# Writing out the order of three engines from a LayerNorm's last sum into the next product, in a two-layer encoder trunk

## The chip, the cores and the metric

The kernel runs on one core of a Trainium2 chip. The metric is the device time of one execution in microseconds (us), the median of several runs. Five engines work side by side, each through its own list of instructions in order: TensorE (PE in the profile; PEld is its weight loads), VectorE (DVE), ScalarE (ACT), GpSimd (POOL) and SyncE (SP), which here only issues DMA transfers.

## What is computed

A sequence of 256 frames of width 2048 goes through two post-norm layers. In short:

```python
h = layer_norm(x, ln_in_g, ln_in_b)
for l in range(2):
    z = h @ w_in[l]                       # queries, keys/values, rope part, conv input u
    u = u + b_glu; c = u[:, :1024] * sigmoid(u[:, 1024:])
    c = silu(layer_norm(depthwise_conv(c, 31 taps)))
    mix = concat([chunk_causal_attention(z), c]) @ w_out[l]
    h = layer_norm(ALPHA * h + mix, ln1_g[l], ln1_b[l])
    f = square(relu(h @ w1[l])) @ w2[l]   # 2048 -> 8192 -> 2048
    h = layer_norm(ALPHA * h + f, ln2_g[l], ln2_b[l])
```

All in float32; positions give the rotary angles of a part of queries and keys.

## The kernel before

**Splitting.** A float32 product is made of three products of a shorter type (float32r): a number is split into hi, its cast, and lo, the rest. ScalarE makes hi, VectorE or GpSimd subtracts to get lo (`split`, L170, and `cutting`, L248, for weights). `stat_x` (L352) then issues, for one 128-row slice `ki`, the products xh·hi, xh·lo, xl·hi into one bank of PSUM.

**Tiling.** The frames are two tiles of 128 (t = 0, 1); the width is four blocks of 512 (n, or kc when it is summed over). A weight chunk is 512 rows by 512 columns (1 MB, four `ki` slices): loaded by SP into a raw buffer `wr`, cut into `wh` and `wl`, used once by each tile t, then dropped. `pump` (L282) keeps a few chunks cut ahead (`ahead`) and some loaded ahead (`cap`), out of 20 big buffers. `gpsimd_low` (L42) says for which chunks GpSimd makes lo.

**Norm.** `accumulate` (L712) adds a product's bank to X and takes the block's statistics; `Norm.head` (L397) aggregates them, with a power on GpSimd (`rstd_of`, L365). `Norm.nrm` (L409) normalises a block in two operations on VectorE (subtract mean and multiply by g; multiply by r and add b), or in two on ScalarE and two on GpSimd. `Norm.turn` (L432) transposes a block on TensorE (four 128x128) and splits the result into xT (tiles `xTa`, `xTb`; `xTi` for the input norm).

**Into the next product.** `close` (L725) writes the last product of a norm's sum; amid it `between` (L727) sums and normalises tile 0's blocks and turns the first. With two chunks of activations (the `wo` case, L741) blocks 2 and 3 are written interleaved, so that tile 0 is summed early. `after_norm` (L448) then writes the other turns and the first product, chunk by chunk. No order is written down there: the scheduler of the build decides how norm, turns, products and cuts of weights are interleaved on each engine. This happens three times: `wo` to `w1` in both layers, and `w2` of layer 0 to `u` of layer 1. The last norm (`N.last`) has no product behind it.

**The opening** (L519 to L581). 24 small products without use (`warm`) come first; x is normalised by a `First` norm (L487) without gain, turned, and gain and bias are applied by ScalarE or VectorE as the turned block leaves PSUM (`gain`, L497; `GV`, L52, lists VectorE's share), into `xv`, which is split into `xTi`. The first product `u` (layer 0, group 0: four chunks, two tiles, banks `u000` and `u001`) follows; then small parameters are transposed (`parameters`, L594: `prmT`, `wdT`), and the product `zq` starts. The small parameters come through SP's queue (L540 to L551), ahead of the fifth weight chunk.

Of the kernel before, what the change touches and what calls it, by code (L numbers as in the profile page):

```python
# [16 lines left out]
P = 128  # L17
D = 2048
S = 256
# [32 lines left out]
GV = {(t, n, k) for t, n in ((1, 0), (1, 1), (0, 2)) for k in range(4)} | {(0, 0, 2), (0, 0, 3)}  # L52
# [24 lines left out]
def hybrid_trunk(ctx: ExitStack, tc: tile.TileContext, x, positions, inv_freq, ln_in_g, ln_in_b,  # L77
# [3 lines left out]
    clock = dict(pe=0.0, dve=0.0)  # L81

    class Counted:

        def __init__(self, eng, key, cost):
            self.eng, self.key, self.cost = eng, key, cost
# [26 lines left out]
    vector = Counted(nc.vector, "dve", dve_cost)  # L113

# [55 lines left out]
    def split(hi, lo, src):  # L170
        return nc.scalar.copy(hi, src), vector.tensor_sub(lo, src, hi.bitcast(F32))  # L171
# [76 lines left out]
    def cutting(pieces):  # L248
# [7 lines left out]
        eng = nc.gpsimd if gpsimd_low(plan[i][0]) else vector  # L256
        for j in range(pieces):
            c = slice(j * m, (j + 1) * m)
            with ExitStack() as order:
# [4 lines left out]
                nc.scalar.copy(hi[:, c], raw[:, c])  # L264
                low = eng.tensor_sub(lo[:, c], raw[:, c], hi[:, c].bitcast(F32))  # L265
                if eng is nc.gpsimd:
                    last["low"] = low
# [97 lines left out]
    def rstd_of(var, eps, scale, name):  # L365
# [3 lines left out]
        nc.gpsimd.tensor_tensor(out=r, in0=v, in1=mhalf, op=ALU.pow)  # L369
        return r  # L370

    class Norm:
        def __init__(self, name, g_ap, b_ap, last=False):
# [5 lines left out]
            self.turned = set()  # L379
# [28 lines left out]

        def nrm(self, t, n, eng=None):  # L409
# [7 lines left out]
            if eng is nc.gpsimd:  # L417
                nc.scalar.activation(X[:, t, c], a, AF.Identity, bias=self.nmu(t), scale=1.0)  # L418
                nc.scalar.activation(X[:, t, c], X[:, t, c], AF.Copy, scale=r)  # L419
# [12 lines left out]
        def turn(self, t, n):  # L432
            if (t, n) in self.turned:
                return
            self.turned.add((t, n))
            while len(self.xT) <= n:
                self.xT.append(v3(big(f"xT{self.name}{len(self.xT)}", F32R), 4))
            xt = self.xT[n]
# [3 lines left out]
            ps = self.gain(ps, t, n)  # L442
            self.cut = split(xt[:, :, t * P:(t + 1) * P], xt[:, :, S + t * P:S + (t + 1) * P], v3(ps, 4))
# [4 lines left out]
    def after_norm(N, keys, ps, lag):  # L448

        def mm(t, kc):  # L450
            hi, lo = get(*keys[kc])
            for ki in range(4):
                stat_x(ps[t], hi, lo, ki, N.xT[kc][:, ki], t, kc == 0 and ki == 0, kc == 3 and ki == 3)
                yield

        state["hold"] = True
        for n in range(3):
            N.nrm(0, n)
            N.turn(0, n)
        N.nrm(1, 0)  # L460
        N.turn(1, 0)
        gate = N.cut
        N.nrm(0, 3)
        N.turn(0, 3)
        for n in range(1, NC4):
            N.nrm(1, n)
            N.turn(1, n)
# [5 lines left out]
        for kc in range(lag):  # L473
            for _ in mm(1, kc):
                pass
            tick()
            retire(*keys[kc])
        for kc in range(lag, NC4):
            for t in range(2):
                for _ in mm(t, kc):  # L480
                    pass
                tick()
            retire(*keys[kc])
        state["gate"] = None


    class First(Norm):  # L487

# [8 lines left out]
        def gain(self, ps, t, n):  # L497
            v = work(f"xv{t}{n}", "ev", 4)
            for k in range(4):
# [4 lines left out]
                else:  # L504
                    nc.scalar.activation(v[:, c], ps[:, c], AF.Identity, bias=b, scale=g)
            return v

# [31 lines left out]
    with nc.allow_non_contiguous_dma(reason="one position a partition"):  # L539
        nc.sync.dma_start(posi, positions[0].rearrange("(t p) -> p t", p=P))  # L540
    nc.sync.dma_start(invf, inv_freq.partition_broadcast(P))
# [3 lines left out]
    for l in range(L):  # L545
        o = l * NR
        for r0, nr, ap in ((0, 16, b_glu), (16, 8, g_cln), (24, 8, b_cln), (32, 8, b_dw)):
            nc.sync.dma_start(prm[o + r0:o + r0 + nr, :], ap[l].rearrange("(r c) -> r c", c=P))
    wdr = big("wdr")
    for l in range(L):  # L550
        nc.sync.dma_start(wdr[:CK, l * CW:(l + 1) * CW], w_dw[l])  # L551
# [3 lines left out]
    nc.scalar.copy(gbT, ps[:, 0:32])  # L555

    def ready_tile(t, n):
        N.nrm(t, n)
        N.turn(t, n)

# [3 lines left out]
    first = cutting(4)  # L564
    next(first)
    next(first)
    ready_tile(0, 0)
    state["gate"] = N.cut[:1]
    beside(first)
    state["gate"] = None  # L570
    ready_tile(0, 1)
    for n in range(NC4):
        N.stats(1, n)
    N.head(1)
    ready_tile(1, 0)
    for n in range(1, NC4):
        for _ in cutting(4):
            pass
        if n + 1 < NC4:
            ready_tile(0, n + 1)  # L580
        ready_tile(1, n)  # L581
# [12 lines left out]
    def parameters():  # L594
# [3 lines left out]
        nc.scalar.copy(pT.rearrange("p l r -> p (l r)"), ps[:, 0:NR * L])  # L598
        nc.scalar.mul(pH.rearrange("p l r -> p (l r)"), ps[:, 0:NR * L], 0.5)
        for l in range(L):  # L600
# [4 lines left out]
            nc.scalar.copy(wdT[:, l].rearrange("p c k -> p (c k)"), ps[:, 0:8 * CK])  # L605
# [28 lines left out]
    def rope_tables():  # L634
        af, tmp = angles[:, 0], angles[:, 3]
        nc.scalar.activation(tmp, af, AF.Abs)
        nc.scalar.activation(sinT.rearrange("p a b -> p (a b)"), af, AF.Sin)
        nc.scalar.activation(cosT.rearrange("p a b -> p (a b)"), tmp, AF.Sin, bias=hpi, scale=-1.0)
# [14 lines left out]
    def convolve(l, i, h, ca):  # L653

        acc = [psumc(f"cv{l}{i}{j}", j)[:, :S] for j in range(2)]
        for j in range(2):
            c = 2 * i + j
            nc.scalar.activation(acc[j], h[:, c], AF.Identity, bias=pT[:, l, 32 + c:33 + c],  # L658
# [9 lines left out]
        for j in range(2):  # L668
            nc.scalar.copy(ca[:, 2 * i + j], acc[j])
# [55 lines left out]
    def close(tag, l, k0, act, N, first=False):  # L725

        def between(i, ps):  # L727
            if i == 0:
                accumulate(0, ps, NC4 - 1, first, N)
                N.head(0)  # L730
                N.nrm(0, 2, nc.gpsimd)
                N.nrm(0, 0)
                N.nrm(0, 1)
            elif not N.last:
                N.turn(0, 0)

        if len(act) > 2:
            for n in range(NC4):
                end = n == NC4 - 1
                ps = out_rows(tag, l, k0, n, act, (3 if N.last else 2) if end else 0, between)  # L740
                for t in range(2):  # L741
                    if t or not end:
                        accumulate(t, ps, n, first, N)
        else:
            for n in range(NC4 - 2):
                ps = out_rows(tag, l, k0, n, act)
                for t in range(2):
                    accumulate(t, ps, n, first, N)
# [516 lines left out]
```

## Time and profile before

| | |
|---|---|
| median of 3 runs | 2019.65 us (2018.78 to 2022.06) |
| the profiled execution's own time | 2019.18 us |
| its span | 2017.4 us |
| busy: TensorE, VectorE, ScalarE, GpSimd | 98%, 61%, 47%, 17% of the span |
| mean granted clock of TensorE | 0.994 of full |
| read from HBM | 373.88 MB, 186 GB/s over the span |

The profile shows one execution. Its page gives busy time by engine and, in 40 slices of the span, the granted clock of TensorE. A timeline has one row for a run of like instructions on an engine: start, length, engine, line, operation, output and inputs, count, and in brackets how long the engine was idle before and what ended that. A matmul's row lasts from its start to its modelled end, so that matmuls overlap: the pace of TensorE is read from start to start. L93 is a helper through which all TensorE and VectorE instructions go.

### The profile page before, as it was taken

Reading aid. Unit: us, or ns where it says so; the run is one execution under the profiler, and the core shown is the slowest. Engines: PE = TensorE matmul, PEld = TensorE weight load, DVE = VectorE, ACT = ScalarE, POOL = GpSimd, SP = SyncE. Lnnn points to the kernel's source line nnn. Section 1 sums busy time; section 2 is a strip of 40 time slices with the busy share of each in tenths; the row PEclk is TensorE's granted clock in tenths of the full one; section 3 lists DMA queues with packets and bytes.
Section 4 is the critical chain, followed back from the end, with each engine's and each line's share of the span. In section 5 each row is a group of like instructions: output and inputs, shape, how many; then the busy total and the mean of one; then the engine's idle time right before and its main releaser. Section 6 shows DMA issues by size and latency. Waiting matters only on the chain. (4 is left out here: it accounts for less than half of the span.)

```text
span 2017.4 us, 26187 instructions
## 1 busy us (share of the span) xinstructions
PE 1984.3 (98%) x10542; PEld 1708.7 (85%) x10542; DVE 1223.8 (61%) x1725; ACT 946.9 (47%) x1341; POOL 333.6 (17%) x208
## 2 busy tenths in 40 slices
PE   7999999999999999999999999999999999999998
PEld 5999878888888888888879997788888888888886
DVE  6875687554555555466567747865555555555564
ACT  5456455543453354344345464555444434543441
POOL 2287902000000000000038764200000000000001
PEclk7999999999999999999999999999999999999999
DMA  7565746456555645657556455455564565556562
GB/s 228 157 168 169 258 170 209 148 196 216 171 188 188 229 154 197 213 168 250 167 168 177 135 178 210 167 187 178 198 217 159 189 198 197 186 190 227 190 221 72
DMA packets 226170, 377.67 MB, mean 187 GB/s; under 512 B 15955, under 2 KB 70083, under 8 KB 225025
## 3 DMA queue, kind: packets, MB, share of 16 engines
q1 hardware_dynamic: 225696, 375.47, 56.7%
q8 instruction: 82, 1.34, 0.3%
q10 hardware_dynamic: 352, 0.54, 0.1%
q14 instruction: 40, 0.32, 0.0%
HBM read 373.88 MB, written 2.10 MB: 186 GB/s over the span
## 5 line engine op out<-in xcount | busy, mean ns | idle before, releaser
L264 ACT CAST wh<-wr 128x1024 fp32r<-128x1024 f32 (+2 forms) x700 | 684.9, 1031 | 745.3 <-DVE wl L93 331.6
L93 DVE TENSOR_TENSOR wl<-wr,wh 128x1024 fp32r<-128x1024 f32 (+1 forms) x592 | 694.9, 1216 | 413.0 <-ACT wh L264 289.5
L93 PE MATMUL w<-wh,h 128*128 128x512 f32 x2048 | 632.0, 389 | 1.5 <-DVE f015s L93 1.5
L93 PE MATMUL f<-xTa,wh 128*128 128x512 f32 x1920 | 454.8, 390 | 0.0
L93 PEld LDWEIGHTS w<-wh,h 128*128 128x128 f32 x2048 | 384.5, 188 | 81.4 <-DVE f015s L93 1.7
L93 PEld LDWEIGHTS f<-xTa,wh 128*128 128x128 f32 x1920 | 354.3, 188 | 70.0
L93 PE MATMUL w<-wl,h 128*128 128x512 f32 x1024 | 398.4, 389 | 0.0
L265 POOL TENSOR_TENSOR wl<-wr,wh 128x1024 fp32r<-128x1024 f32 (+1 forms) x108 | 245.1, 2294 | 85.5 <-ACT wh L264 31.4
L93 PEld LDWEIGHTS f<-xTa,wl 128*128 128x128 f32 x1920 | 243.7, 191 | 7.9
L93 PE MATMUL f<-xTa,wl 128*128 128x256 f32 x1920 | 247.3, 283 | 0.0
L369 POOL TENSOR_TENSOR rb<-vb,mhalf 128x1 f32<-128x1 f32 x4 | 3.7, 924 | 1387.0 <-DVE nmub L93 1387.0
L93 PEld LDWEIGHTS w<-wl,h 128*128 128x128 f32 x1024 | 192.3, 188 | 39.5
L93 DVE SCALAR_TENSOR_TENSOR cv<-hg,wdT,cv 128x255 f32<-128x255 f32 (+14 forms) x480 | 187.3, 464 | 11.3 <-ACT cv L658 11.3
L93 PE MATMUL wo<-wh,mx 128*128 128x512 f32 x256 | 82.7, 396 | 1.0 <-ACT mx L171 1.0
L93 PE MATMUL wo<-wh,mc 128*128 128x512 f32 x256 | 79.7, 390 | 0.0
L93 PE MATMUL u<-xTi,wh 128*128 128x256 f32 x384 | 71.4, 286 | 0.0
L93 PE MATMUL u<-xTb,wh 128*128 128x256 f32 x384 | 71.2, 286 | 0.0
L93 DVE TENSOR_TENSOR X<-X,w 128x512 f32<-128x512 f32 x44 | 30.3, 688 | 64.6 <-PE w L93 64.6
L93 PEld LDWEIGHTS u<-xTi,wh 128*128 128x128 f32 x384 | 60.3, 192 | 0.2
L93 PEld LDWEIGHTS u<-xTb,wh 128*128 128x128 f32 x384 | 60.2, 191 | 0.2
L93 PEld LDWEIGHTS wo<-wh,mx 128*128 128x128 f32 x256 | 48.0, 188 | 11.3 <-ACT mx L171 1.5
L93 PEld LDWEIGHTS wo<-wh,mc 128*128 128x128 f32 x256 | 48.1, 188 | 9.9
(403 smaller groups left out, 1811.4 us busy)
## 6 DMA issues: line engine op xcount, KB each, us to landing
wr<-in_w_dram SPq DMA_DIRECT2D x256, 1024.0 KB, 5.2
wr<-in_w_out_dram SPq DMA_DIRECT2D x32, 1024.0 KB, 5.3
wr<-in_w_in_dram SPq DMA_DIRECT2D x60, 512.0 KB, 4.3
wr<-in_w_in_dram SPq DMA_DIRECT2D x8, 1024.0 KB, 11.1
wr<-in_w_uq_dram SPq DMA_DIRECT2D x24, 256.0 KB, 4.3
wr<-in_w_in_dram SPq DMA_DIRECT2D x8, 640.0 KB, 4.1
wr<-in_w_ukv_dram SPq DMA_DIRECT2D x8, 512.0 KB
wr<-in_w_in_dram SPq DMA_DIRECT2D x16, 128.0 KB, 4.8
```

The costliest lines, as they stand in the source:

```text
L93: return f(*args, **kw)
L264: nc.scalar.copy(hi[:, c], raw[:, c])
L265: low = eng.tensor_sub(lo[:, c], raw[:, c], hi[:, c].bitcast(F32))
L369: nc.gpsimd.tensor_tensor(out=r, in0=v, in1=mhalf, op=ALU.pow)
```

## The change

1. A helper (`Counted`) can now chain an engine's instructions in the order in which the program text writes them (`chained`, through `issue_after`), and ScalarE goes through it too. The chain is on for TensorE, VectorE and ScalarE from `between(0)` (or from the opening's start) to the end of the written sequence.
2. `after_norm` is one written sequence. A token is an operation: `f`, `s` the two halves of the norm of block (t, n), `t` its transposes, `p` its split, `a`, `b` the two halves of its product (six matmuls each), `m` all of it, `c` half a cut of the fourth chunk, `x` the rest of it. A turn stands amid a product's twelve matmuls. ScalarE and GpSimd no longer normalise, except in the last norm.
3. `close` no longer has the interleaved `wo` case: tile 0's last two chunks of block 3 come first, then tile 1's.
4. The opening is written in order likewise. The first two chunks of `u` are not cut: their 16 matmuls take the unsplit float32 `xv` and raw weights (16 where 48 were). `GV` gives ScalarE more of the gains.
5. The small loads move from SP's queue to GpSimd's, behind the second power of the input norm; `prmT` and `wdT` wait for the opening's last matmul, the angles for a later power, the rope tables for a later ScalarE instruction.
6. The key rope's transposes move behind `u` group 2; lo of layer 1's `u` group 1 moves from GpSimd to VectorE.

```diff
@@ gpsimd_low, GV, Counted
     if tag == "u":
-        return key[2] >= 2 - l
+        return key[2] >= 2
...
-GV = {(t, n, k) for t, n in ((1, 0), (1, 1), (0, 2)) for k in range(4)} | {(0, 0, 2), (0, 0, 3)}
+GV = {(t, n, k) for t, n in ((1, 1), (1, 3)) for k in range(4)}
...
                 clock[self.key] += self.cost(op, args, kw)
-                return f(*args, **kw)
+                with ExitStack() as order:
+                    if self.key in chained and self.prev is not None:
+                        order.enter_context(tc.issue_after(self.prev.ins))
+                    self.prev = f(*args, **kw)
+                return self.prev
@@ after_norm
-        for n in range(3):
-            N.nrm(0, n)
-            N.turn(0, n)
...
-        for kc in range(lag):
-            for _ in mm(0, kc):
-                pass
-            tick()
-        state.update(hold=False, gate=gate)
...
+        fourth = cutting(2, True)
...
+        for w in ("a00 t01 p01 b00 f02 s02 a01 t02 f10 p02 s10 b01 f11 s11 a02 t10 p10 b02 f12 s12 a10 t11 p11 b10 f03 s03 "
+                  "c a11 t12 p12 b11 c f13 s13 a12 t03 p03 b12 x a03 t13 p13 b03 m13").split():
...
+            if w == "x":
...
+                state["gate"] = (scalar.prev, vector.prev)
...
+        chained.clear()
+        state["hold"] = False
+        pump(index[keys[3]] + 3)
@@ opening
-    nc.sync.dma_start(invf, inv_freq.partition_broadcast(P))
...
-    first = cutting(4)
...
-    for n in range(1, NC4):
-        for _ in cutting(4):
-            pass
-        if n + 1 < NC4:
-            ready_tile(0, n + 1)
-        ready_tile(1, n)
+    chained.update(("pe", "dve", "act"))
...
+            if kc < 2:
+                tensor.matmul(ups[t], lhsT=N.v[t, kc][:, ki * P:(ki + 1) * P], rhs=raw[kc][1][:, ki],
+                              start=kc == 0 and ki == 0, stop=False)
+            else:
+                stat_x(ups[t], *ready[index["u", 0, 0, kc]], ki, N.xT[kc][:, ki], t, False, kc == 3 and ki == 3)
...
+    for step in ("n00 n01 t00 t01 m00 n02 n03 t02 s0 s1 s2 s3 h p00 t03 p01 a01 n10 n11 t10 b01 n12 n13 p02 p03 a10 c2 c2 "
+                 "t11 b10 c2 c2 p10 c3 c3 a11 t12 b11 c3 c3 p12 a02 t13 b02 p11 m12 m03 p13 m13").split():
...
+    small.enter_context(tc.issue_after(last["pow"].ins))
+    for l in range(L):
+        nc.gpsimd.dma_start(wdr[:CK, l * CW:(l + 1) * CW], w_dw[l])
...
+            nc.gpsimd.dma_start(prm[o + r0:o + r0 + nr, :], ap[l].rearrange("(r c) -> r c", c=P))
@@ close, between
+                if not N.last:
+                    state["hold"] = True
+                    chained.update(("pe", "dve", "act"))
                 accumulate(0, ps, NC4 - 1, first, N)
                 N.head(0)
-                N.nrm(0, 2, nc.gpsimd)
-                N.nrm(0, 0)
-                N.nrm(0, 1)
...
+                    for n in range(2):
+                        N.first(0, n)
+                    for n in range(2):
+                        N.second(0, n)
             elif not N.last:
                 N.turn(0, 0)
+                N.parts(0, 0)
@@ layers
         if l == 0:
-            parameters()
+            with tc.issue_after(opened.ins):
+                parameters()
```

**TensorE in the opening.** Names: `tri` and two digits is the turn of block (t, n); `u000`, `u001` the banks of tiles 0 and 1; `wr` raw, `wh`/`wl` cut weights. Before:

```order
L93 MATMUL gbT_158<-ident_109,gbr_106 128x32
L93 MATMUL tri00_179<-ident_109,X_70 128x128 x4
L93 MATMUL tri01_197<-ident_109,X_70 128x128 x4
L93 MATMUL tri02_244<-ident_109,X_70 128x128 x4
L93 MATMUL u000_344<-wh0_171,xTi0_178 128x512
L93 MATMUL u000_344<-wl0_172,xTi0_178 128x512
L93 MATMUL u000_344<-wh0_171,xTi0_178 128x512 x2
...
L93 MATMUL u000_344<-wh1_232,xTi1_196 128x512
L93 MATMUL tri10_220<-ident_109,X_70 128x128 x4
L93 MATMUL tri11_257<-ident_109,X_70 128x128 x4
L93 MATMUL tri03_281<-ident_109,X_70 128x128 x4
```

Now:

```order
L98 MATMUL gbT_146<-ident_109,gbr_106 128x32
L98 MATMUL tri00_163<-ident_109,X_70 128x128 x4
L98 MATMUL tri01_173<-ident_109,X_70 128x128 x4
L98 MATMUL u000_159<-wr0_114,xv00_168 128x512 x4
L98 MATMUL tri02_189<-ident_109,X_70 128x128 x4
L98 MATMUL tri03_212<-ident_109,X_70 128x128 x4
L98 MATMUL u000_159<-wr1_127,xv01_178 128x512 x2
L98 MATMUL tri10_229<-ident_109,X_70 128x128 x4
L98 MATMUL u000_159<-wr1_127,xv01_178 128x512 x2
L98 MATMUL u001_160<-wr0_114,xv10_234 128x512 x2
L98 MATMUL tri11_257<-ident_109,X_70 128x128 x4
L98 MATMUL u001_160<-wr0_114,xv10_234 128x512 x2
```

The product no longer waits for the split: it starts behind two turns, on raw weights and `xv`, and turns stand between halves of products instead of in groups of three behind two whole chunks.

**GpSimd in the opening**, now, behind the two powers of the input norm (before, none of these loads stood in this list):

```order
L377 TENSOR_TENSOR ri0_157<-vi0_155,mhalf_71 128x1
L377 TENSOR_TENSOR ri1_207<-vi1_205,mhalf_71 128x1
L636 DMA wdr_144<-in_w_dw_dram 31x1024
L639 DMA gbr_106<-in_b_glu_dram 16x128
L639 DMA gbr_106<-in_g_cln_dram 8x128
L639 DMA gbr_106<-in_b_cln_dram 8x128
L639 DMA gbr_106<-in_b_dw_dram 8x128
L636 DMA wdr_144<-in_w_dw_dram 31x1024
L639 DMA gbr_106<-in_b_glu_dram 16x128
L639 DMA gbr_106<-in_g_cln_dram 8x128
L639 DMA gbr_106<-in_b_cln_dram 8x128
L639 DMA gbr_106<-in_b_dw_dram 8x128
```

Ten loads stand in one row there; TensorE's `prmT` and `wdT` need them, and stand ahead of `zq`.

**TensorE from `wo` to `w1` in layer 0.** `tra0` and two digits is the turn of block (t, n), `wo0_8_3_1` the last bank of the sum (tile 1), `f000` the next product's bank of tile 0. Before:

```order
L93 MATMUL wo0_8_3_1_3041<-wh44_2941,mc01_2329 128x512
L93 MATMUL tra000_3085<-ident_109,X_70 128x128 x4
L93 MATMUL tra001_3123<-ident_109,X_70 128x128 x4
L93 MATMUL tra002_3131<-ident_109,X_70 128x128 x4
L93 MATMUL f000_3120<-wh45_2973,xTa00_3084 128x512
L93 MATMUL f000_3120<-wl45_2974,xTa00_3084 128x512
L93 MATMUL f000_3120<-wh45_2973,xTa00_3084 128x512 x2
```

Now:

```order
L98 MATMUL wo0_8_3_1_2955<-wh44_2888,mc01_2277 128x512
L98 MATMUL tra000_3025<-ident_109,X_70 128x128 x4
L98 MATMUL wo0_8_3_1_2955<-wh44_2888,mc01_2277 128x512
L98 MATMUL wo0_8_3_1_2955<-wl44_2889,mc01_2277 128x512
L98 MATMUL wo0_8_3_1_2955<-wh44_2888,mc01_2277 128x512 x2
L98 MATMUL wo0_8_3_1_2955<-wl44_2889,mc01_2277 128x512
L98 MATMUL wo0_8_3_1_2955<-wh44_2888,mc01_2277 128x512
L98 MATMUL f000_3046<-wh45_2920,xTa00_3024 128x512
L98 MATMUL f000_3046<-wl45_2921,xTa00_3024 128x512
```

The first turn moved ahead of the last six matmuls of the sum, and the second behind the first six of the next product; three turns in a row stood there before.

**VectorE at the same place** (`X<-X,mva00,ga0` is the first half of a block's norm, `X<-X,ra00,ba0` the second, `xTa00<-tra000` a split's lo, `X<-X,wo0_8_3_1` the last sum). Before:

```order
L93 SCALAR_TENSOR_TENSOR X_70<-X_70,mva00_3025,ga0_2786 128x512 x3
L93 BN_STATS sta01_2785<-X_70 128x6
L93 SCALAR_TENSOR_TENSOR X_70<-X_70,ra00_3029,ba0_2787 128x512 x3
L93 TENSOR_TENSOR X_70<-X_70,wo0_8_3_1_3041 128x512
L93 BN_STATS sta01_2785<-X_70 128x6
L93 TENSOR_TENSOR xTa00_3084<-tra000_3085,xTa00_3084 128x4x128
L93 TENSOR_TENSOR xTa01_3122<-tra001_3123,xTa01_3122 128x4x128
L93 BN_AGGR mva01_3100<-sta01_2785 128x2
```

Now:

```order
L98 SCALAR_TENSOR_TENSOR X_70<-X_70,mva00_2996,ga0_2734 128x512 x2
L98 SCALAR_TENSOR_TENSOR X_70<-X_70,ra00_3000,ba0_2735 128x512 x2
L98 TENSOR_TENSOR xTa00_3024<-tra000_3025,xTa00_3024 128x4x128
L98 TENSOR_TENSOR X_70<-X_70,wo0_8_3_1_2955 128x512
L98 BN_STATS sta01_2733<-X_70 128x6
L98 BN_AGGR mva01_3040<-sta01_2733 128x2
L98 TENSOR_SCALAR va01_3042<-mva01_3040 128x1
L98 TENSOR_TENSOR xTa01_3058<-tra001_3059,xTa01_3058 128x4x128
L98 SCALAR_TENSOR_TENSOR X_70<-X_70,mva00_2996,ga0_2734 128x512
L98 SCALAR_TENSOR_TENSOR X_70<-X_70,ra00_3000,ba0_2735 128x512
L98 SCALAR_TENSOR_TENSOR X_70<-X_70,mva01_3040,ga0_2734 128x512
L98 TENSOR_TENSOR xTa02_3080<-tra002_3081,xTa02_3080 128x4x128
```

The first split's lo now stands ahead of the last sum, and each further split between norm halves of later blocks.

## Rows read from the trace of the kernel before

**Rows 1.** The page: span, and TensorE's share

```profile
span 2017.4 us, 26187 instructions
...
PE 1984.3 (98%) x10542; PEld 1708.7 (85%) x10542; DVE 1223.8 (61%) x1725; ACT 946.9 (47%) x1341; POOL 333.6 (17%) x208
```

**Rows 2.** Windows, opening: length; busy PE, PEld, DVE, ACT, POOL (x); clock; DMA share, GB/s

```profile
12.60:22.70 10.10, 7.95 (x20) 6.00 (x21) 7.82 (x16) 4.11 (x9) 3.42 (x8) 0.50 0.93 289
...
26.20:29.50 3.30, 0.24 (x2) 0.24 (x3) 3.30 (x9) 1.75 (x4) 2.79 (x6) 1.00 0.50 90
29.70:39.80 10.10, 7.98 (x24) 6.04 (x23) 7.32 (x16) 9.10 (x24) 0.93 (x3) 0.50 0.95 311
```

**Rows 3.** Costliest TensorE groups from 8.6 to 54.6 us: busy, mean ns, idle before

```profile
L93 PE MATMUL u<-wh,xTi 128*128 128x512 f32 x64 | 24.9, 469 | 0.9 <-DVE xTi L93 0.9
L93 PE MATMUL u<-wl,xTi 128*128 128x512 f32 x32 | 14.8, 464 | 0.0
L93 PE MATMUL tri<-ident,X 128*128 128x128 f32 x32 | 6.2, 340 | 7.4 <-DVE xv L93 7.2 <-DVE X L93 0.2
```

**Rows 4.** Timeline of the opening: start, length, engine line op, idle before

```profile
6.78 1.28 ACT L264 ACT_TABLE_LOAD   x1 [6.78 <-DMA wr<-in_w_in_dram]
...
8.43 1.91 DVE L93 TENSOR_SCALAR X<-X,mvi,ri 128x512 f32<-128x512 f32 x4 [0.67 <-POOL ri L369]
...
9.89 2.21 ACT L505 ACTIVATE xv<-tri,gbT 128x128 f32<-128x128 f32 x6
...
13.57 1.87 DVE L93 BATCH_NORM_STATS2 sti<-X 128x6 f32<-128x512 f32 x3
...
16.31 2.18 ACT L264 CAST wh<-wr 128x512 fp32r<-128x512 f32 x4 [0.96 <-DMA wr<-in_w_in_dram]
...
22.66 0.58 POOL L369 TENSOR_TENSOR ri<-vi,mhalf 128x1 f32<-128x1 f32 x1
...
24.66 1.03 PE L93 MATMUL tri<-ident,X 128*128 128x128 f32 x8
```

**Rows 5.** Timeline, TensorE after the opening: product at full clock, then zq

```profile
43.29 1.07 PE L93 MATMUL u<-wh,xTi 128*128 128x512 f32 x4
44.20 0.39 PE L93 MATMUL u<-wl,xTi 128*128 128x512 f32 x1
...
53.36 1.18 PE L93 MATMUL wdT<-ident,wdr 31*128 31x31 f32 x16
...
54.66 0.47 PE L93 MATMUL zq<-wh,xTi 128*128 128x512 f32 x1
```

**Rows 6.** Timeline, TensorE in attention: float32 products, two records each

```profile
179.62 0.59 PE L93 MATMUL sc<-qr 128*128 128x256 f32 x2
180.06 0.59 PE L93 MATMUL sc<-kn,qn 128*128 128x256 f32 x2
```

**Rows 7.** Timeline, SP queue: issues of the small loads

```profile
17.93 1.71 SPq L548 DMA_DIRECT2D gbr<-in_b_glu_dram  x1
...
22.52 0.27 SPq L548 DMA_DIRECT2D gbr<-in_g_cln_dram  x1
```

**Rows 8.** The three turns from norm to product, by stretch (columns as rows 2)

```profile
306.37:312.86 6.49, 4.99 (x28) 3.80 (x26) 6.01 (x12) 3.10 (x6) 1.51 (x2) 1.00 1.03 382
1018.48:1025.34 6.86, 5.23 (x28) 3.78 (x26) 6.62 (x11) 2.62 (x5) 2.99 (x3) 1.00 1.06 383
1296.51:1302.91 6.40, 5.20 (x27) 3.79 (x26) 6.33 (x11) 2.42 (x5) 2.35 (x3) 1.00 1.03 384
```

**Rows 9.** Timeline of the middle one: last sum, the two norm halves

```profile
1013.24 0.69 DVE L93 TENSOR_TENSOR X<-X,w 128x512 f32<-128x512 f32 x1 [6.19 <-PE w L93]
...
1015.11 2.07 DVE L93 SCALAR_TENSOR_TENSOR X<-X,mvb,gb 128x512 f32<-128x512 f32 x3
...
1017.10 4.13 DVE L93 SCALAR_TENSOR_TENSOR X<-X,rb,bb 128x512 f32<-128x512 f32 x3
1017.10 1.89 POOL L420 TENSOR_TENSOR X<-X,gb 128x512 f32<-128x512 f32 x1 [0.83 <-ACT X L419]
```

More of the change, by code (lines that the diff above doesn't have):

```diff
@@ L80, in hybrid_trunk @@
     nc = tc.nc
-    clock = dict(pe=0.0, dve=0.0)
+    clock = dict(pe=0.0, dve=0.0, act=0.0)
+    chained = set()
     class Counted:
         def __init__(self, eng, key, cost):
-            self.eng, self.key, self.cost = eng, key, cost
+            self.eng, self.key, self.cost, self.prev = eng, key, cost, None
         def __getattr__(self, op):
@@ L368, in rstd_of @@
         r = sm.tile([P, 1], F32, name=f"r{name}", tag="r")
[L369 removed]
+        last["pow"] = nc.gpsimd.tensor_tensor(out=r, in0=v, in1=mhalf, op=ALU.pow)
         return r
@@ L378, in __init__ @@
             self.done = set()
-            self.turned = set()
+            self.read = {}
             self.xT = []
@@ L563, in hybrid_trunk, with whole @@
     N.head(0)
-    first = cutting(4)
[L565 to L576, printed above, removed]
-        for _ in cutting(4):
-            pass
-        if n + 1 < NC4:
-            ready_tile(0, n + 1)
-        ready_tile(1, n)
+    ups = [psum(f"u00{t}") for t in range(2)]
+    def whole():
+        i = state["cut"]
+        state["cut"] += 1
+        (a, b), _ = plan[i][1]
+        return i, v3(raws.pop(i)[:, :a * b], a)
@@ new lines, in hybrid_trunk @@
+    for step in ("n00 n01 t00 t01 m00 n02 n03 t02 s0 s1 s2 s3 h p00 t03 p01 a01 n10 n11 t10 b01 n12 n13 p02 p03 a10 c2 c2 "
+                 "t11 b10 c2 c2 p10 c3 c3 a11 t12 b11 c3 c3 p12 a02 t13 b02 p11 m12 m03 p13 m13").split():
+        a, b = [int(i) for i in (step[1:] + "00")[:2]]
+        if step[0] == "s":
+            N.stats(1, a)
+        elif step == "h":
+            N.head(1)
+        elif step[0] == "c":
+            next(chunk[a])
+        elif step[0] in "mab":
+            product(a, b, dict(m=range(4), a=(0, 1), b=(2, 3))[step[0]])
+        else:
+            dict(n=N.nrm, t=N.turn, p=N.parts)[step[0]](a, b)
@@ new lines, in hybrid_trunk @@
+    for c in chunk.values():
+        beside(c)
+    chained.clear()
+    opened = tensor.prev
+    small = ExitStack()
+    small.enter_context(tc.issue_after(last["pow"].ins))
+    for l in range(L):
+        nc.gpsimd.dma_start(wdr[:CK, l * CW:(l + 1) * CW], w_dw[l])
+        o = l * NR
+        for r0, nr, ap in ((0, 16, b_glu), (16, 8, g_cln), (24, 8, b_cln), (32, 8, b_dw)):
+            nc.gpsimd.dma_start(prm[o + r0:o + r0 + nr, :], ap[l].rearrange("(r c) -> r c", c=P))
+    with nc.allow_non_contiguous_dma(reason="one position a partition"):
+        nc.gpsimd.dma_start(posi, positions[0].rearrange("(t p) -> p t", p=P))
@@ L762, in close @@
+                N.parts(0, 0)
+        for n in range(NC4):
+            end = n == NC4 - 1
+            ps = out_rows(tag, l, k0, n, act, (3 if N.last else 2) if end else 0, between)
+            for t in range(2):
+                if t or not end:
+                    accumulate(t, ps, n, first, N)
         N.head(1)
-        for n in range(1, NC4):
-            if not N.last or n == 2:
-                N.nrm(1, n, nc.gpsimd)
+        if N.last:
+            N.nrm(1, 2, nc.gpsimd)
     for l in range(L):
```

275 lines of the change are left out of this document (147 added, 128 removed).

## The prediction

> **What bounds the kernel now.** I read the page first. TensorE is busy for 98% of the span [rows 1], so nothing but time that TensorE loses can be won: its idle time, its time at half clock, and its own work. The profiled execution took 2019.18 us, 0.47 below the median of 2019.65; every sum is made against it. Next I read TensorE's pace from start to start: four 512-column products of the split type take 44.20 - 43.29 = 0.91, so 0.2275 us each at full clock [rows 5]. Where the distance between two starts is longer, time is lost. That happens in two kinds of places which the change touches.
>
> First the opening. The windows show the granted clock at 0.50 from 12.6 to 22.7 and from 29.7 to 39.8, that is 1.2 instead of 2.4 GHz [rows 2]. Ahead of these falls TensorE stood: its turns waited 7.2 us for `xv`, the gained block that leaves PSUM [rows 3], and from 26.2 to 29.5 it was busy for 0.24 us of 3.3 [rows 2]. Gain, normalisation and cut of the second tile are made in long runs on VectorE and ScalarE, and three turns stand in a row behind them. The first product's last matmul ends at 53.36, and `zq` starts at 54.66 behind `wdT`, 16 small transposes of 1.18 us in all [rows 5].
>
> Second, the three places where a norm meets the next product. The windows from the first turn to the first half product show 6.49, 6.86 and 6.40 us [rows 8]; each holds twelve transposes and fourteen products. Four transposes take about 0.5 us (eight took 1.03 [rows 4]), so the work is 1.5 + 14 x 0.2275 = 4.7, and 1.8, 2.2 and 1.7 are lost, 5.7 together. VectorE and ScalarE are the reason: the timeline of the middle one shows three second halves of the norm at 4.13 us while GpSimd normalised too, against 2.07 for three first halves [rows 9].
>
> **The opening, added up.** Only the chain of the new order is needed, with durations of these rows. VectorE normalises the first two blocks from 8.43 on, 0.48 each [rows 4]. ScalarE's table load of 1.28 us [rows 4] now falls behind the first small transpose, so that its first gain starts at about 10.4; a gain takes 2.21 / 6 = 0.37 [rows 4]. The product therefore starts at about 10.9. What TensorE has then to do: sixteen unsplit products, which appear as two records of 256 columns in attention at 180.06 - 179.62 = 0.44 for 256 columns [rows 6], so 0.88 for 512, 14.1 together; 48 split ones at 0.2275, 10.9; six turns of 0.5, 3.0. That is 28.0, or 38.9 without a wait. (Sixteen unsplit products replace 48 split ones; this alone costs 14.1 - 10.9 = 3.2.) I see two waits. The second raw chunk lands at 16.3 (the cut in the rows waited for it until then [rows 4]), when TensorE, with four products and two more turns done, has been ready since about 15.3: 1.0. The turn of tile 1's first block needs its normalisation. Its statistics, four of 0.62, can start at about 12.3, and GpSimd's power of 0.58 [rows 4] is done at about 16.6. But in VectorE's list two splits now stand ahead of it, and they need ScalarE: two runs of four gains and two casts of 0.55 to 0.6 (four casts took 2.18 [rows 4]), to 19.1; then a lo of about 0.69 [rows 9] and 0.48: 20.3. TensorE ran dry at 18.0, so 2.4. With both waits the last matmul ends at 42.3. Twelve more handovers between engines are not counted; I take **43**. `zq` follows 1.6 later as before (`prmT`, `wdT` and the two transposes of `uT` between): 44.6 against 54.66. Gain **10.1**. By the bounds of no wait at all (38.9) and no half clock avoided (one fall, below) it lies between 14.2 and 5.
>
> **The small loads.** They leave SP's queue, which frees it for the fifth chunk, and ten of them stand on GpSimd behind the power at 16.6. TensorE's `prmT` and `wdT` now wait for them directly ahead of `zq`, and behind `zq` everything is queued. No row shows a load issued by GpSimd. On SP their issue took 0.27 to 1.71 us [rows 7]; ten at 1.71 would be issued by 33.7, and 5 us more to land still end before 43. So I cost them at nothing; the cover is gone at (43 - 16.6 - 5) / 10 = 2.1 us each. The angles, on the same queue, are needed much later.
>
> A page speaks against this part. The Trainium skill, "SBUF — State Buffer", sections "SBUF: two separate sides" and "A bandwidth-pool intuition that's wrong (but worth ruling out)", says that a transfer issued by GpSimd starves for its descriptors while VectorE runs an operation in a two-port mode: about 3.1 us instead of 0.62. By that figure ten loads would land at about 52.6 and the total would be some 9.6 us above the sum below; no run here shows it yet.
>
> **The three boundaries.** The last sums of tile 0, their statistics, power and two blocks' norm (0.69 + 0.7 + 1.4 for two first halves, the power beside them, + 1.4 for two second ones [rows 9]) take 4.2 us, and TensorE has 18 products, 4.1 us, before the first turn, now put before the last six matmuls of the sum: a wait near zero. From there a turn and twelve products, 0.5 + 12 x 0.2275 = 3.2 us, alternate. In that time VectorE has a first half, a second half and a lo, 3 x 0.69 = 2.1 us with GpSimd quiet, and about 0.65 of waiting for ScalarE's cast: 2.7. So TensorE should set the pace. I leave 0.3 per place for handovers: 5.7 - 0.9 = **4.8** gained, between 0 (another wait in its place) and 6.5 (losses behind the window go as well). The interleaved end of `wo` that is removed had given tile 0's sum its lead; the new order of the last two chunks gives it the same. The cut of the fourth chunk in halves, the shifted cuts behind it and the last split of tile 1, which stands behind five cuts, cost nothing as long as later chunks' products lie between; ScalarE, which no longer normalises, has that time. Moving the key rope's transposes and one group's lo from GpSimd to VectorE (61% busy [rows 1]) costs nothing either.
>
> **Sum:** 2019.18 - 10.1 - 4.8 = **2004.3**.
>
> **Rivals.**
> *B, the clock falls once more in the opening.* TensorE was idle in stretches ahead of both falls [rows 2, 3], and the new order keeps idle times of 1.0 and 2.4 us. One stretch of 10.1 us at half clock costs at most 5.1 of work, less the about 1 us of wait that it covers: 4. Total 2008.3; with nothing gained at the boundaries 2013.1. Against: no idle stretch of the new chain is as long as the 3.3 in the rows.
> *C, the loads are late.* VectorE's second halves took twice as long beside GpSimd [rows 9]; if GpSimd's issues suffer alike, 1.71 doubles to 3.4: the last lands at 16.6 + 34 + 5 = 55.8, 12.8 after the need, total 2017. Below 2.1 us each it vanishes; from 4.1 each the kernel is slower than before. Only the long one of the SP rows speaks for it, the short one (0.27) against.
> *D, slower: VectorE's turn outlasts TensorE's.* In the written order VectorE's lo waits for ScalarE's cast and blocks the norm halves behind it: 0.5 transposes + 0.6 cast + 0.69 lo + 2 x 0.69, and four handovers of 0.2 to 0.3, 4.2 us in the worst case against 3.2. Seven turns at three places lose 21: 2025.3. It costs time above 3.2 per turn and makes the kernel slower than before from 3.9. Against: one turn's transposes lie beside the former one's lo, so that not all of it is in series.
> *E, the boundaries give nothing, the opening all:* a chunk's cut, now behind norm and turn on chained engines, comes late and takes the gain. 2009.1.
>
> **How the numbers follow.** Chances: the forecast (opening at full clock, boundaries won) 0.50, B 0.20, E 0.10, C 0.12, D 0.08. The likeliest gives 2004.3. The range holds the forecast, B and E, 0.80: from 2001 (opening end at 42, boundaries 6.5) to 2013 (B without boundaries). About 0.2%, 4 us, can be told from no change, so "same" is 2015.6 to 2023.7: C for the most part, and a mild D, 0.09; slower is the rest of D and a C beyond 4 us each, 0.07; faster the rest, 0.84.
>
> **What would show it.** Right: in the changed profile the clock stays 1.00 through the opening, the first product ends near 43 and `zq` starts near 44.6, with less than 0.5 us idle before `prmT`; the tile 1 turn waits about 2 us at 18 to 20; windows over the three boundaries show under 0.5 us of idle each. Wrong: a slice at 0.50 (B); TensorE idle before `prmT` or `wdT`, released by a DMA (C); TensorE idle before each turn's product, released by VectorE's lo, over and over (D); idle behind the boundary released by a cut (E). If the unsplit product takes more than 0.88, each 0.06 above it adds 1 us.

## The result and the profile after

| | before | changed |
|---|---|---|
| median | 2020.4 us (4 runs) | 2005.46 us (2004.27 to 2006.79, 4 runs) |
| ratio | | 0.993, interval 0.9917 to 0.9942 |
| the profiled execution | 2019.18 us | 2004.81 us, span 2002.8 us |

It is faster, by 14.9 us between the medians and 14.4 between the profiled executions. The forecast was 2004.3.

The opening, in windows: from the first product to the wait for the second raw chunk, that wait, and from there to the product's end (columns as in [rows 2]).

```profile
10.30:14.90 4.60, 4.57 (x16) 2.38 (x16) 1.53 (x4) 2.81 (x9) 0.00 (x0) 1.00 0.91 297
14.90:17.30 2.40, 0.01 (x1) 0.01 (x1) 2.28 (x5) 2.40 (x8) 0.62 (x1) 1.00 0.89 240
17.30:41.10 23.80, 23.25 (x88) 15.11 (x89) 19.17 (x32) 17.27 (x31) 9.07 (x17) 1.00 1.05 344
```

The clock stays at 1.00 where it had been 0.50 for 20 us [rows 2]. Two waits of TensorE remain; its timeline has them in brackets, and the end:

```profile
10.34 3.70 PE L98 MATMUL u<-wr,xv 128*128 128x512 f32 x8
...
17.32 1.95 PE L98 MATMUL u<-wr,xv 128*128 128x512 f32 x4 [2.41 <-DMA wr<-in_w_in_dram]
...
19.80 0.63 PE L98 MATMUL tri<-ident,X 128*128 128x128 f32 x4 [0.53 <-DVE X L98]
...
41.12 0.23 PE L98 MATMUL prmT<-ident,gbr 80*128 80x80 f32 x1
41.28 1.18 PE L98 MATMUL wdT<-ident,wdr 31*128 31x31 f32 x16
42.39 0.50 PE L98 MATMUL zq<-wh,xTi 128*128 128x512 f32 x1
```

`prmT` follows the product without a bracket: the loads on GpSimd were there. Their issues, from GpSimd's timeline:

```profile
17.62 0.75 POOL L636 DMA_DIRECT2D wdr<-in_w_dw_dram  x1
18.38 0.53 POOL L639 DMA_DIRECT2D gbr<-in_b_glu_dram  x1
...
24.46 0.51 POOL L639 DMA_DIRECT2D gbr<-in_b_cln_dram  x1 [2.56 <-DMA wdr<-in_w_dw_dram]
24.96 0.50 POOL L639 DMA_DIRECT2D gbr<-in_b_dw_dram  x1
```

Half a microsecond or a little more each, a stop of 2.56 behind the eighth until the first had landed, and by the trace the tenth landed at 30.2, 10.9 ahead of `prmT`.

The three boundaries, each from the first turn to the fourth (in the first and the third, TensorE's only bracket is 0.17 us):

```profile
293.88:303.84 9.96, 9.79 (x49) 7.89 (x49) 7.70 (x13) 1.76 (x3) 0.55 (x1) 1.00 1.00 350
1007.10:1017.09 9.99, 9.91 (x50) 7.92 (x50) 7.82 (x13) 1.76 (x3) 0.55 (x1) 1.00 0.86 312
1282.12:1292.14 10.02, 9.85 (x49) 7.88 (x49) 7.72 (x13) 1.76 (x3) 0.55 (x1) 1.00 1.01 353
```

Twelve transposes and 36 products are 1.5 + 36 x 0.2275 = 9.7, so 0.3 is lost in each, where 1.8, 2.2 and 1.7 had been over a shorter stretch, with 14 products [rows 8]. A turn comes every 3.2 to 3.5 us.

One place became worse, the one ahead of `w2` in layer 0. Before the change:

```profile
931.30 0.50 PE L93 MATMUL w<-wh,h 128*128 128x512 f32 x1 [1.50 <-DVE f015s L93]
```

In the changed kernel:

```profile
915.46 1.99 ACT L272 CAST wh<-wr 128x1024 fp32r<-128x1024 f32 x2 [8.76 <-DMA wr<-in_w_dram]
...
916.54 2.36 DVE L273 TENSOR_TENSOR wl<-wr,wh 128x1024 fp32r<-128x1024 f32 x2 [8.40 <-ACT wh L272]
...
918.81 0.74 DVE L98 TENSOR_TENSOR f015s<-f,f015s 128x256 f32<-128x256 f32 x2
...
919.62 0.50 PE L98 MATMUL w<-wh,h 128*128 128x512 f32 x1 [2.38 <-DVE f015s L98]
```

```profile
920.35:923.77 3.42, 3.42 (x9) 2.65 (x9) 2.74 (x5) 2.51 (x6) 0.00 (x0) 0.50 0.40 157
```

The last two blocks are the timeline of three engines and a window of what follows (columns as in [rows 2]). `f015s` is the reading of the last MLP block out of its banks; the `w` product stands until VectorE has made it. In VectorE's list it comes behind the cut of a chunk that landed at 915.4. TensorE stands for 2.38 us where it had been 1.50, and from 0.7 us after that the clock is at half for 3.4 us, which it is not at this place in the trace before.

### The profile page after: what moved, and what is told of

It is laid out like the page before. It is cut to its first block, busy times and chain, and to the rows that moved or that the text cites. A ratio compares the mean times of both kernels' runs of the same rounds, so it can differ in the third digit from the quotient of the medians.

```text
span 2002.8 us, 26087 instructions
## 1 busy us (share of the span) xinstructions
PE 1979.2 (99%) x10526; PEld 1701.3 (85%) x10526; DVE 1230.6 (61%) x1737; ACT 928.5 (46%) x1315; POOL 284.1 (14%) x192
## 4 chain that ended last, share of the span: by engine, by line
PE 89%; DVE 2%; DMA 1%; ACT 1%; POOL 0%; issue 0%; POOLq 0%; ACTq 0%; SPq 0%
PE w L98 35%; PE f L98 34%; PE wo L98 8%; PE u L98 6%; PE zq L98 1%; PE sc L98 1%; DVE cv L98 1%; PE zk L98 1%; DMA wr<-in_w_dram 1%; PE qn L98 1%; ACT wh L272 1%; DMA wr<-in_w_out_dram 1%; PE pv L98 0%; PE tra L98 0%; POOL wl L273 0%
## 5 line engine op out<-in xcount | busy, mean ns | idle before, releaser
L272 ACT CAST wh<-wr 128x1024 fp32r<-128x1024 f32 (+1 forms) x678 | 669.6, 1041 | 724.8 <-DVE wl L273 321.6
L273 DVE TENSOR_TENSOR wl<-wr,wh 128x1024 fp32r<-128x1024 f32 x578 | 680.7, 1221 | 413.7 <-ACT wh L272 283.2
L273 POOL TENSOR_TENSOR wl<-wr,wh 128x1024 fp32r<-128x1024 f32 (+1 forms) x100 | 226.6, 2288 | 70.0 <-ACT wh L272 26.0
```

The costliest lines, as they stand in the source:

```text
L272: act.copy(hi[:, c], raw[:, c])
L273: low = on.tensor_sub(lo[:, c], raw[:, c], hi[:, c].bitcast(F32))
```

## The experiments

Each gives its ratio to the kernel before, run on the same chip; the changed kernel's is 0.993. Where lost time is named, it is counted over TensorE's rows from start to start, beyond 0.2275 us for a product. A trace shows one execution; where that one lies well off the median, the text says so.

**1. The new opening alone.**

```diff
-def after_norm(N, keys, ps):      # written sequence
+def after_norm(N, keys, ps, lag): # as before, close and turn too
```

> The new opening with the three boundaries as before. Theory (two gains that add): zq starts at 42.4 as in the changed kernel, 12 us earlier than before; the three boundaries lose 8.3 us together as before; total about 2008 (2006 to 2010). Rival (the opening is nearly all of it, the boundaries' written order is worth under 1 us): 2005 to 2006. Second rival (the time won in the opening is waited for later, because the weights come no sooner): above 2012.

Measured: 2009.08 us, ratio 0.9955 (0.9938 to 0.9971). `zq` starts at 43.15, 0.8 later than in the changed kernel: in this trace the clock is at half from 18.03 to 21.44, behind the wait for the second raw chunk (2.03). The three boundaries lose 2.8, 3.1 and 2.8 us, 8.7 together where the kernel before had 8.3. The wait ahead of `w2` is the old one (1.49). The opening gives 11 of the 15 us, and little of it is waited for later: 0.61 us ahead of `u` at 113.66, for a lo of GpSimd's (0.62 in the changed kernel, none before).

**2. The boundaries alone.** The opening and the small loads are as before.

```diff
+                if not N.last:
+                    state["hold"] = True
+                    chained.update(("pe", "dve", "act"))
...
+        if l:
+            after_norm(N, keys, ps)
+        else:
+            first_norm(N, keys, ps, 1)
```

`first_norm` is the old `after_norm`, for the first product alone.

> The three boundaries in written order with the opening as before. Theory: zq at 54.7, TensorE loses about 1.1 us at each boundary instead of 2.5 to 3.1, total about 2015 (2014 to 2017). Rival (written order at the boundaries is worth nothing): 2019 to 2021.

Measured: 2014.46 us, ratio 0.9977 (0.9967 to 0.9986). The boundaries lose 1.2, 1.0 and 1.2, and the wait ahead of `w2` is longer than before with half clock behind it (3.7 lost there, 1.8 before). (The trace is of an execution of 2016.3. In it `zq` starts at 53.42, 1.2 earlier than in the trace before, though the lists of the opening are the same: the first stretch at half clock is 6.8 us long instead of 10.2.) The two parts give 10.9 and 5.6 by their medians (2020.03 for the kernel before), 16.5 together against 14.9; with intervals of 3.3 and 1.9 us to either side this is no difference. The wait ahead of `w2` is longer than before (1.84 to 2.38) in every trace with the new boundaries but that of experiment 7 and the two made to shorten it.

**3. The loads ahead of GpSimd's powers.** The order tie of the ten loads was moved:

```diff
-    small.enter_context(tc.issue_after(last["pow"].ins))
+    small.enter_context(tc.issue_after(opened.ins))
```

> The changed kernel with GpSimd's small loads issued behind the opening's last product matmul. In the changed kernel the first is issued at 17.6 and the last of the ten lands at 30.2, 12.6 later. Theory (they are hidden there and stand on TensorE's path once the cover is gone): prmT and wdT wait about 12 us behind 41, released by a DMA, total about 2018. Rival (TensorE finds other work or the loads go faster when VectorE is quieter): below 2010.

Measured: 2010.88 us, ratio 0.9958 (0.9943 to 0.9972), but not what was meant. Tied to an instruction of TensorE instead of one of GpSimd's own, the loads were not held, and went to the head of GpSimd's list:

```profile
1.32 0.74 POOL L636 DMA_DIRECT2D wdr<-in_w_dw_dram  x1 [0.34 <-issue]
...
8.36 0.51 POOL L639 DMA_DIRECT2D gbr<-in_b_cln_dram  x1 [2.37 <-DMA wdr<-in_w_dw_dram]
...
11.16 0.59 POOL L377 TENSOR_TENSOR ri<-vi,mhalf 128x1 f32<-128x1 f32 x1
```

```profile
10.83:17.65 6.82, 5.26 (x12) 3.08 (x13) 4.23 (x8) 2.90 (x8) 0.90 (x2) 0.50 0.89 264
24.48:31.30 6.82, 6.02 (x11) 2.95 (x12) 4.52 (x9) 4.90 (x11) 0.00 (x0) 0.50 0.96 335
```

The first power came at 11.16 instead of 7.88, the first turn at 12.39 instead of 9.06, and in two stretches of the windows the clock fell to 0.50. TensorE's, VectorE's and ScalarE's lists are those of the changed kernel. `zq` starts at 50.84: 3.3 us of delay at the start became 8.5. This is rival B, brought about by another late start. The tie to the second power is worth 5.4 us by the medians; the trace is of the slowest of the four executions (2012.67).

**4. The first two chunks cut.**

```diff
-    raw = [whole() for _ in range(2)]
-    chunk = {kc: cutting(4, True) for kc in (2, 3)}
+    chunk = {kc: cutting(4, True) for kc in range(4)}
```

> The changed kernel with the first two chunks of u cut, 48 matmuls where 16 unsplit ones are; the written order gets their cuts. Theory (the unsplit product costs TensorE 3.2 us but takes eight casts of 0.55 us and eight low halves of 0.64 off ScalarE and VectorE, which set the pace there): first product matmul at 14 to 15 instead of 10.3, end of the product 2 to 6 us later than 41.1, total 2008 to 2012, more if the granted clock falls to 0.5 in the opening again. Rival (TensorE's own work sets the end): 3 us earlier, 2002.

The cuts of the two chunks are written into the opening's order.

Measured: 2011.84 us, ratio 0.9965 (0.9952 to 0.9978), the total that the theory had. In TensorE's timeline:

```profile
14.14 0.79 PE L98 MATMUL u<-wh,xTi 128*128 128x512 f32 x1 [4.08 <-ACT xTi L98]
...
22.04 0.50 PE L98 MATMUL u<-wh,xTi 128*128 128x512 f32 x1 [2.19 <-ACT wh L98]
```

The product starts 3.8 later and waits for casts, the clock falls again (11.2 to 18.0, and 35.1 to 38.5), and `zq` starts at 51.34. The product ends 9.0 later than in the changed kernel, beyond the 2 to 6 of the theory, which had left the clock out; the trace is of the slowest of the five executions (2013.57). By the medians the unsplit product saves 6.4 us, though it gives TensorE 3.2 more to do.

**5. No chain in the opening.** 

```diff
-    chained.update(("pe", "dve", "act"))
     for n in range(NC4):
         N.stats(0, n)
```

> The changed kernel without the chain in the opening: the text, the unsplit chunks and GpSimd's loads stay, the scheduler orders each engine. Theory (the written order is part of the gain: with turns pulled ahead the product waits for gains again): the product ends 2 to 5 us later than 41.1, total 2007.5 to 2010.5. Rival (what wins there is the unsplit product and the loads' place, not the chain): 2005 to 2006.5.

Measured: 2000.93 us (2000.67 to 2004.43), ratio 0.9914 (0.9899 to 0.9929). The theory fell, and the rival's 2005 to 2006.5 lies above the result too. TensorE takes three turns together, and in the trace the product ends 1.3 earlier:

```profile
9.22 1.63 PE L98 MATMUL tri<-ident,X 128*128 128x128 f32 x12 [0.26 <-DVE X L98]
16.74 1.96 PE L98 MATMUL u<-wr,xv 128*128 128x512 f32 x4 [2.02 <-DMA wr<-in_w_in_dram]
...
39.90 1.18 PE L98 MATMUL wdT<-ident,wdr 31*128 31x31 f32 x16
41.01 0.50 PE L98 MATMUL zq<-wh,xTi 128*128 128x512 f32 x1
```

The profiled execution is the one of 2004.43, and it has the wait ahead of `w2` (2.24 us). The other three are 3.5 us faster; which wait they lack, no trace shows.

**6. No chain at the boundaries.**

```diff
                     state["hold"] = True
-                    chained.update(("pe", "dve", "act"))
```

> The changed kernel without the chain at the three boundaries; the text's order of turns, products and norm halves stays and the scheduler may reorder. Theory (the chain makes the turns stand amid products): TensorE loses 2 to 3 us at each boundary again, total 2009 to 2011. Rival (the text's order and a GpSimd that no longer normalises suffice): 2005 to 2006.5.

Measured: 2017.7 us, ratio 0.999 (0.9981 to 1.0), beyond what the theory gave. VectorE's timeline in the middle boundary:

```profile
1008.43 2.73 DVE L98 SCALAR_TENSOR_TENSOR X<-X,mvb,gb 128x512 f32<-128x512 f32 x4
...
1011.08 2.73 DVE L98 SCALAR_TENSOR_TENSOR X<-X,rb,bb 128x512 f32<-128x512 f32 x4
...
1014.33 2.35 DVE L98 TENSOR_TENSOR wl<-wr,wh 128x1024 fp32r<-128x1024 f32 x2
...
1016.60 0.68 DVE L98 TENSOR_TENSOR xTb<-trb,xTb 128x512 fp32r<-128x512 f32 x1
...
1017.34 1.22 PE L98 MATMUL u<-wh,xTb 128*128 128x512 f32 x2 [2.24 <-DVE xTb L98]
```

With VectorE doing all norms, the scheduler lets it do four first and four second halves in a row, and a cut, ahead of the lo that the product waits for. The boundaries lose 5.2, 6.9 and 5.4, more than before the change.

**7. The small loads on SP.** They stand there ahead of a weight chunk again, as before the change.

```diff
-        nc.gpsimd.dma_start(wdr[:CK, l * CW:(l + 1) * CW], w_dw[l])
+        nc.sync.dma_start(wdr[:CK, l * CW:(l + 1) * CW], w_dw[l])
...
-            nc.gpsimd.dma_start(prm[o + r0:o + r0 + nr, :], ap[l].rearrange("(r c) -> r c", c=P))
+            nc.sync.dma_start(prm[o + r0:o + r0 + nr, :], ap[l].rearrange("(r c) -> r c", c=P))
```

> The changed kernel with the ten small loads on SP's queue again, ahead of the fourth and fifth weight chunk. Before, these issues filled 8 us of that queue. Theory (moving them matters because the weights behind them are issued late): the cuts of the opening's later chunks or of zq's wait for a DMA, total 2008 to 2011. Rival (the weights come early enough either way): 2005 to 2006.5.

Measured: 2010.29 us, ratio 0.9958 (0.9943 to 0.9973). SP's queue and, below, ScalarE and TensorE:

```profile
22.39 0.22 SPq L578 DMA_DIRECT2D wdr<-in_w_dw_dram  x1
26.85 0.32 SPq L581 DMA_DIRECT2D gbr<-in_b_glu_dram  x1
29.63 0.27 SPq L581 DMA_DIRECT2D gbr<-in_g_cln_dram  x1
32.83 0.27 SPq L581 DMA_DIRECT2D gbr<-in_b_cln_dram  x1
33.15 0.29 SPq L581 DMA_DIRECT2D gbr<-in_b_dw_dram  x1
33.49 20.98 SPq L251 DMA_DIRECT2D wr<-in_w_in_dram  x12
```

```profile
53.08 1.99 ACT L272 CAST wh<-wr 128x1024 fp32r<-128x1024 f32 x2 [3.81 <-DMA wr<-in_w_in_dram]
...
55.99 0.41 PE L98 MATMUL uT<-ident,ut 128*128 128x128 f32 x2 [2.97 <-DVE ut L98]
```

The first two issues (at 17.41 and 18.20) take 0.7 and 1.2 us, the others 0.2 to 0.4, but between them the queue stands for up to 4.2. The next weight chunk is issued at 33.5, against 17.9 in the changed kernel, and behind 46 the cuts and TensorE wait for it. By the medians the move is worth about 5 us. In the trace the price in the opening is higher: at `wo` of layer 0 TensorE is 8.3 us behind the changed kernel, and it wins about 3 back ahead of `w2`, where it stands for 0.93 instead of 2.38 and the clock stays up.

**8. The cuts behind the bank reads, ahead of `w2`.**

```diff
+                if kc == 3 and l == 0 and g == NG - 1:
+                    state["hold"] = True
...
+            if l == 0 and g == NG - 1:
+                state["hold"] = False
+                state["gate"] = tuple(added)
```

`added` is VectorE's last bank read.

> The changed kernel with one more order: at the end of layer 0's first MLP product the cuts of three later chunks stand behind the reading of its banks, on ScalarE and VectorE. In the changed kernel TensorE stands 2.38 us there behind a VectorE that cuts a late-landing chunk, and runs at half clock for 3.4 us behind that; with only the opening changed it stands 1.7. Theory (that wait is the cut's place on VectorE and gives back part of the boundaries' gain): under 1 us of idle there, no half clock, total 2002 to 2003.5. Rival (the cuts come late then and the products of w2 wait for them): 2005 to 2008.

Measured: 2000.54 us (2000.27 to 2001.4), ratio 0.9909 (0.9894 to 0.9924). In VectorE's and TensorE's timeline nothing is late there any more:

```profile
915.56 0.76 DVE L98 TENSOR_TENSOR f015s<-f,f015s 128x256 f32<-128x256 f32 x2 [10.61 <-ACT f015s L98]
...
917.89 0.40 PE L98 MATMUL w<-wh,h 128*128 128x512 f32 x1
```

The 4.2 us lost there in the changed kernel are gone, and no wait for the later cuts came in their place. The total is 1.5 us below the theory's range: the ratios differ by what the place loses, 0.0021 or 4.2 us, and the theory had counted on 2 to 3.5.

**9. Experiments 5 and 8 together,** both diffs.

> The changed kernel without the chain in the opening and with the cuts behind the bank reads before w2 (the two versions that came out faster than the changed kernel). Theory (they act at two places, 41 and 917, and add): zq starts near 41, no idle above 1 us before w2, total 1998 to 2000. Rival (what the version without the opening's chain gained is the same wait before w2, which only the profiled run showed): 2000 to 2001, as the second alone.

Measured: 2000.44 us (2000.1 to 2000.71), ratio 0.9902 (0.9888 to 0.9917). The rival's total holds: it is as fast as 8 alone. That the three faster executions of experiment 5 lacked the wait ahead of `w2` fits this, and is not shown. `zq` starts at 42.85 in the trace, 1.8 later than in that of experiment 5, but the clock is at half in a window of it (columns as in [rows 2]), and at no place of the opening in the trace of experiment 5:

```profile
17.91:21.32 3.41, 3.41 (x9) 1.76 (x8) 2.73 (x5) 0.71 (x3) 3.18 (x7) 0.50 1.03 338
```

So whether the 1.3 us of experiment 5 come each time stays open; the medians of this experiment and of 8 show nothing of them. It is the lowest ratio measured, and no different from that of 8 within their intervals; experiment 10 ran on the same chip, has the changed kernel's order ahead of `w2`, and its runs (2003.88 and more) don't overlap these.

**10. The small loads held back.** A copy on GpSimd that reads the last block's split stands ahead of them.

```diff
-    small.enter_context(tc.issue_after(last["pow"].ins))
+    after13 = nc.gpsimd.tensor_copy(late, N.xT[3].bitcast(F32)[:, 0, S + P:S + P + 1])
+    small.enter_context(tc.issue_after(after13.ins))
```

> The changed kernel with the ten small loads held on GpSimd until the last block's split is made (34.8 in the changed kernel; a copy of one column there reads it). In the changed kernel they take 12.6 us from the first issue (17.6) to the last landing (30.2), 10.9 ahead of the need. Theory (hidden only by that lead): they land at about 47.4, TensorE waits about 6 us before prmT or wdT, total 2011 to 2013. Rival (off the path, or faster there): 2005 to 2007.

Measured: 2005.05 us, ratio 0.9927 (0.9912 to 0.9941), the time of the changed kernel. The loads are issued from 35.79 on, and the tenth lands at 47.7. But the scheduler, which knew of the copy, put the start of `zq` (41.87) ahead of `wdT`, and the second half of `wdT` (49.59) and `prmT` (50.72) further back:

```profile
42.32 0.39 PE L98 MATMUL zq<-wh,xTi 128*128 128x512 f32 x1
42.64 0.68 PE L98 MATMUL wdT<-ident,wdr 31*128 31x31 f32 x8
43.25 0.50 PE L98 MATMUL zq<-wh,xTi 128*128 128x512 f32 x1
```

So the lead of 10.9 us wasn't what kept the loads off the path here: `zq` doesn't need `prmT`, and TensorE's list moved. What the loads cost with TensorE's list as it was, the run doesn't show.

**11 and 12. Chains on some engines.** At the boundaries, on TensorE alone, and on VectorE and ScalarE alone.

```diff
-                    chained.update(("pe", "dve", "act"))
+                    chained.update(("pe",))           # 11
+                    chained.update(("dve", "act"))    # 12
```

> The changed kernel with only TensorE chained at the three boundaries. Theory (without any chain VectorE was given four first and four second norm halves in a row, and cuts, ahead of the lo that the product waits for; VectorE's order is what matters): TensorE stands longer still, now in the written order, total 2015 to 2022. Rival (the turns' place on TensorE is what matters): 2005 to 2008.

Measured: 2024.44 us, ratio 1.0023 (1.0014 to 1.0033): slower than before the change, and by 2 us more than I had expected. The first boundary, timeline of VectorE and TensorE:

```profile
292.47 2.73 DVE L98 SCALAR_TENSOR_TENSOR X<-X,mva,ga 128x512 f32<-128x512 f32 x4
...
295.12 2.35 DVE L98 TENSOR_TENSOR wl<-wr,wh 128x1024 fp32r<-128x1024 f32 x2
297.39 2.73 DVE L98 SCALAR_TENSOR_TENSOR X<-X,ra,ba 128x512 f32<-128x512 f32 x4
...
298.28 1.09 PE L98 MATMUL tra<-ident,X 128*128 128x128 f32 x4 [3.59 <-DVE X L98]
```

> The changed kernel with only VectorE and ScalarE chained at the three boundaries, TensorE left to the scheduler. Theory (VectorE's order is what matters): TensorE loses 1 to 2 us at each boundary, total 2005 to 2009. Rival (TensorE's order is what matters): 2012 to 2018.

Measured: 2010.28 us, ratio 0.9951 (0.9936 to 0.9966). The boundaries lose 3.05, 3.04 and 3.05, no less than before the change, where I had expected 1 to 2 each; the total is 1 us beyond my 2005 to 2009. The order of VectorE and ScalarE decides most of what lies between experiment 6 and the changed kernel: fixing it wins 7 of these 12 us by the medians, and fixing TensorE's alone makes it worse. TensorE's order on top of it wins the other 5. Against the kernel before, neither wins anything at the boundaries by itself: the gain of 5 us needs both. VectorE's order without ScalarE's was not run.

## Why the prediction was right, and where its steps were off

**The opening: right in kind, 2 us too small.** The product started at 10.34 (10.9 was worked out), and TensorE had its two waits, 2.41 and 0.53 where I had 1.0 and 2.4: the raw chunk came at 17.3, 1.0 later than in the rows, and tile 1's block was normalised 0.7 earlier. Together they are 2.9 against 3.4. The step that was off in both starts is ScalarE's table load: I had put it behind the first small transpose, and it ran at 2.6, so that the gains began at 9.82 instead of 10.4. The product ended at 41.1, where the chain had 42.3 and I took 43 for handovers that cost nothing. `zq` came at 42.39: 12.3 instead of 10.1, 0.2 of it because `uT` is now behind. The half clock did not come in this trace, and that was in part luck: it came once, for 3.4 us, in the traces of experiments 1, 9, 10, 11 and 12, from 17.6 to 18.3 on, behind the same wait for the second raw chunk (1.96 to 2.38 there). With the changed kernel's opening, `zq` started at 43.15 to 43.37 in the traces that have it (1, 11, 12) and at 42.33 to 42.45 in those that don't (6, 8 and the changed kernel's). So rival B's mechanism does act, at a cost of 0.7 to 1 us for a stretch of 3.4, where I had put 4 for one of 10.1; experiments 3 and 4 show what it takes back when the product starts 4 us late.

**What carries the opening is not the order alone.** The prediction gave the gain to "the new order". The chain is not needed for it (experiment 5). The unsplit product (6.4 us by experiment 4) and the loads' place on GpSimd behind the powers (about 5 by the medians of 3 and of 7) are; I had costed the loads at nothing, which was right for their landing, and had named SP's freed queue without a price. These three prices don't add: they come to 16.6, where the opening gives 11.

**The small loads: right.** Issues of 0.50 to 0.75 us, within my bounds of 0.27 to 1.71, and no wait at `prmT`. Rival C did not come. By the Trainium skill, "SBUF — State Buffer", section "SBUF: two separate sides", such loads starve while VectorE runs a two-port operation. GpSimd's issues stayed at 0.51 us while VectorE normalised four blocks (19.07 to 21.15) in the changed kernel, and the last load, which the prediction had at 52.6 by that page's figure, landed at 30.2; no run here shows which of VectorE's operations take both ports.

**The boundaries: right, with its size.** 0.3 lost per place was left, and 0.3 is measured; 5.7 - 0.9 = 4.8 in the stretch, and 5.0 over the whole of each place (8.3 lost before, 3.3 now). TensorE sets the pace with 3.2 to 3.5 us per turn, as worked out; rival D needs VectorE's order to fail, and with TensorE alone in a written order (experiment 11) it did, and the kernel was slower than before.

**What the prediction missed** is the wait ahead of `w2`: 2.4 us more are lost there, 0.9 of it a longer wait and 1.5 the half clock behind it. That is rival E's mechanism (a late cut in front of a waiting read) at a place 600 us behind the boundary. The sum of what the trace shows is 12.1 + 5.0 - 2.4 = 14.7, and 14.4 was measured between the profiled executions; that the prediction's 14.9 agrees so closely is luck: 2 us too little in the opening and 2.4 too few in losses cancel.

## What to carry to other kernels

Where several engines hand blocks round, write down the order of the engines that feed the bound one first, and then that of the bound one: a written TensorE list behind an unordered VectorE made things worse than no order at all, and at the boundaries a gain over the kernel before came only with both. Where the bound engine waits for preparation (casts, cuts) at a start, let it take the longer form that needs none: 3.2 us more on TensorE bought 6.4 here. After each such change look for the next wait far from the edit: the place ahead of `w2` gave 4 to 5 us for a few lines.

## What the runs showed that was not expected

Short stretches at half clock follow single waits of TensorE in some executions and not in others: 3.4 us after the wait of 2.38 ahead of `w2`, none after the 2.41 at 14.9 of the same execution. Over all traces, the waits of 1.84 to 2.38 us ahead of `w2` were followed by such a stretch in eight of nine, those of 0.93 to 1.50 in none of three; the waits for the second raw chunk were followed by one five times (1.96 to 2.38 us) and not by one five times (1.57 to 2.74 us). So the length of the wait alone doesn't tell. Small loads on SP held up their queue for far longer than their issue: 0.2 to 1.2 us each, yet 16 us until the next weight load was issued (17.4 to 33.5), while GpSimd's list stopped once among the ten, for 2.56.
